# One first store of ten tokens, or two of five, in a mixture-of-experts combine

## The chip, the cores and the metric

The kernel runs on one core of a Trainium2 chip. The metric is device time in microseconds (us) of one execution. Three executions of the kernel before took 239.29, 239.32 and 239.38 us, median 239.32 us. All the other numbers of the kernel before come from one further execution, taken by the hardware profiler.

## The reference

For 16 x 1024 = 16384 tokens there are two expert outputs of 512 floats each and two weights. The result is their weighted sum:

```python
weights = combine_weights[..., np.newaxis]
return np.sum(expert_outputs * weights, axis=2).astype(np.float32)
```

Shapes: `expert_outputs` (16, 1024, 2, 512), `combine_weights` (16, 1024, 2), result (16, 1024, 512), all float32. Two floats are read for each float written: 67.24 MB are read and 33.56 MB written.

## The kernel before

The tokens are laid over the 128 partitions, 128 tokens to each. Tokens 0 to 117 of every partition come from the first part of the input and tokens 118 to 127 from the rest (`LAST`, line 35, and `rows`, line 40). A token takes 4 KB of input and 2 KB of result in its partition.

The partition's 128 tokens are cut into eleven tiles, numbered 0 to 10, of 10, 12, 12, ..., 12 and 10 tokens (`TILES`, line 30). Four rooms in one SBUF tile `et` hold them: tile g lies in room g mod 4 (`ROOMS`, line 29). So tile 4 takes the room of tile 0, tile 5 that of tile 1, and so on.

Three things happen to a tile:

- A load (`load`, line 68, issued on line 71) is one DMA on the queue of SyncE (SP). It has 128 rows, one for each partition; a row of a 12-token tile is 48 KB. Tile 0 alone comes in two loads, of 2 and of 8 tokens (`FIRST`, line 31). The profile calls this queue q1.
- The combine (`combine`, line 76) runs on VectorE (DVE). For tiles 0 to 8 it is one multiply of the whole tile by the broadcast weights (line 83) and one add of the two halves (line 90), which writes the result into the front half of the same room. In tile 9 ScalarE (ACT) does half of the multiplies (lines 87 and 89). In tile 10 ACT and DVE go token by token (lines 95 and 96).
- A store (line 121) is one DMA for each entry of `STORES` (line 32): one each for tiles 0 to 6, one for tiles 7 and 8 together and one for tiles 9 and 10. Stores 0 to 6 are issued by ACT, on its own queue, which the profile calls q10; a row of a 12-token store is 24 KB and a row of store 0 is 20 KB. The last two stores are issued by SP (line 120) and so stand on q1 behind the loads.

After the store of a tile the loop issues the load of the tile four further on (line 124). It takes the same room, so SP waits until that store has wholly landed before it issues the load. SP works its loads strictly in the order of the tiles; while it waits for one store, nothing behind it on SP is issued.

Each DMA signals its end on one of eight completion counters, which the build hands out in turn. A DMA that gets a used counter waits for the counter's previous DMA.

The order of the instructions on each engine is that of the program (`manual_schedule`, line 100). Ahead of the loop stand a small store of zeros (line 104), the two loads of weights (line 74, on q10) and a warm-up of ACT (line 107).

Of the kernel before, what the change touches and what calls it, by code (L numbers as in the profile page):

```python
# [1 line left out]

# [4 lines left out]


@with_exitstack
def kernel(  # L10
    ctx: ExitStack,
    tc: tile.TileContext,
    expert_outputs: bass.AP,
    combine_weights: bass.AP,
    out: bass.AP,
):

    nc = tc.nc
    b, s, k, h = expert_outputs.shape
    assert k == 2
    n = b * s
    P = nc.NUM_PARTITIONS
    per = n // P
    assert per * P == n

    ROOM, ROOMS = 12, 4
    TILES = [10, 12, 12, 12, 12, 12, 12, 12, 12, 12, 10]  # L30
    FIRST = [2, 8, 12, 12, 12]
    STORES = [[0], [1], [2], [3], [4], [5], [6], [7, 8], [9, 10]]
    WHOLE = [0, 1, 2, 3, 4, 5, 6, 7, 8]
    MIXED = [9]
    LAST = 118
    assert sum(TILES) == per and [g for st in STORES for g in st] == list(range(len(TILES)))
    main = per - LAST
    starts = [sum(TILES[:g]) for g in range(len(TILES))]

    def rows(x):  # L40

        first = x[0 : P * main, :].rearrange("(p t) f -> p t f", p=P)
        second = x[P * main : n, :].rearrange("(p t) f -> p t f", p=P)
        return lambda t, c: first[:, t : t + c, :] if t < main else second[:, t - main : t - main + c, :]

    flat = out.rearrange("b s h -> (b s) h")
    eo = rows(expert_outputs.rearrange("b s k h -> (b s) (k h)"))
    cw = rows(combine_weights.rearrange("b s k -> (b s) k"))
    o = rows(flat)

    dt = mybir.dt.float32
    mult = mybir.AluOpType.mult
    add = mybir.AluOpType.add
    copy = mybir.ActivationFunctionType.Copy

    pool = ctx.enter_context(tc.tile_pool(name="all", bufs=1))
    et = pool.tile([P, ROOMS * ROOM, k * h], dt)
    halves = et.rearrange("p j (k h) -> p (j k) h", k=k)
    wt = pool.tile([P, per * k], dt)
    wk = wt.rearrange("p (t k) -> p t k", k=k)  # L60
    zt = pool.tile([16, 128], dt)
    warm = pool.tile([P, 1], dt)

    def place(t):
        g = max(g for g in range(len(TILES)) if starts[g] <= t)
        return g % ROOMS * ROOM + t - starts[g]

    def load(t, c, **kw):
        at = place(t)
        assert place(t + c - 1) == at + c - 1  # L70
        nc.sync.dma_start(out=et[:, at : at + c], in_=eo(t, c), **kw)  # L71

    def weights(q, t, c):
        q.dma_start(out=wk[:, t : t + c, :], in_=cw(t, c))

    def combine(g, base):
        at, c, t0 = g % ROOMS * ROOM, TILES[g], starts[g]
        if g in WHOLE or g in MIXED:
            room = halves[:, k * at : k * (at + c), :]
            x0, x1 = et[:, at : at + c, 0:h], et[:, at : at + c, h : 2 * h]  # L80
            if g in WHOLE:
                wb = wt[:, k * t0 : k * (t0 + c)].unsqueeze(2).to_broadcast([P, k * c, h])
                nc.vector.tensor_tensor(out=room, in0=room, in1=wb, op=mult)  # L83
            else:
                for i in range(c):
                    x = et[:, at + i, 0:h]
                    nc.scalar.activation(out=x, in_=x, func=copy, scale=wt[:, k * (t0 + i) : k * (t0 + i) + 1])  # L87
                w1 = wk[:, t0 : t0 + c, 1:2].to_broadcast([P, c, h])
                nc.vector.tensor_tensor(out=x1, in0=x1, in1=w1, op=mult)  # L89
            nc.vector.tensor_tensor(out=halves[:, base : base + c, :], in0=x0, in1=x1, op=add)  # L90
            return
        for i in range(c):
            t = k * (t0 + i)
            x0, x1 = halves[:, k * (at + i), :], halves[:, k * (at + i) + 1, :]
            nc.scalar.activation(out=x0, in_=x0, func=copy, scale=wt[:, t : t + 1])  # L95
            nc.vector.scalar_tensor_tensor(  # L96
                out=halves[:, base + i, :], in0=x1, scalar=wt[:, t + 1 : t + 2], in1=x0, op0=mult, op1=add
            )

    with tc.manual_schedule():  # L100
        nc.vector.memset(zt, 0.0)  # L101

        ahead = flat[0 : P * main, :].rearrange("(q t) h -> q (t h)", q=16)
        nc.scalar.dma_start(out=ahead[:, 0:128], in_=zt)  # L104
        weights(nc.scalar, 0, main)
        weights(nc.scalar, main, per - main)
        nc.scalar.activation(out=warm, in_=nc.const_aps.tensor(1.0, (P, 1), dt), func=copy)  # L107

        t = 0
        for i, c in enumerate(FIRST):  # L110
            load(t, c, **({"max_dma_last_dim": k * h * 4} if i == 0 else {}))
            t += c
        assert t == sum(TILES[:ROOMS])
        for j, st in enumerate(STORES):
            base, c = st[0] % ROOMS * ROOM * k, 0
            for g in st:
                combine(g, base + c)
                c += TILES[g]
            assert c <= k * ROOM
            q = nc.sync if j in (7, 8) else nc.scalar  # L120
            q.dma_start(out=o(starts[st[0]], c), in_=halves[:, base : base + c, :])
            for g in st:
                if g + ROOMS < len(TILES):
                    load(starts[g + ROOMS], TILES[g + ROOMS])


# [1 line left out]
_INS = ['expert_outputs', 'combine_weights']  # L128
_OUTS = [((16, 1024, 512), 'float32')]


# [23 lines left out]
```

## Time and profile before

| | |
|---|---|
| median of three executions | 239.32 us (239.29 to 239.38) |
| span of the profiled execution, first to last instruction | 237.6 us |
| what an execution has around the span (median less span) | 1.7 us |
| DVE busy | 192.1 us, 81% of the span |
| ACT busy | 15.2 us, 6% |
| DMA moved | 100.80 MB, mean 424 GB/s |

How to read it. The span runs from the first to the last instruction, and all times in the views are counted from its start. The core has 16 DMA engines that move the rows of all DMAs; a record of one row is called a packet. A DMA of 128 rows gives each engine 8 rows, and at its end 16 markers of 4 bytes, one for each engine, which raise the completion counter. So a DMA of 128 rows shows as 144 packets. A queue's share is the time that its packets took, as a share of the time of all 16 engines. "Landing" is the time from the issue of a DMA until its counter is full.

### The profile page before, as it was taken

The numbers are of one execution on the slowest core, as the hardware profiler recorded it, in microseconds if no ns is written. First come the engines' busy times: TensorE is split into PE (matmuls) and PEld (weight loads), VectorE is DVE, ScalarE is ACT, GpSimd is POOL, SyncE is SP. The second block draws the span as 40 slices with busy tenths as digits, with TensorE's granted clock in tenths as the row PEclk, the third lists the DMA queues.
The fourth block names the chain that finished last, engine by engine and source line by source line (L and its number), as shares of the span: only waits on it lengthen the run. The fifth ranks groups of instructions, "written<-read, shape, count | busy, mean of one in ns | idle before, by whom it ended". The sixth has DMA issues, their size and how long they took to land.

```text
span 237.6 us, 154 instructions
## 1 busy us (share of the span) xinstructions
DVE 192.1 (81%) x31; ACT 15.2 (6%) x24; POOL 0.2 (0%) x4
## 2 busy tenths in 40 slices
DVE  0039999999999996998799699969987999998000
ACT  2000000000000000000000000000000008482000
POOL 0000000000000000000000000000000000000000
DMA  7999998999999999999999999999999999999895
GB/s 266 442 445 405 456 481 375 375 430 477 439 447 414 397 405 455 463 397 430 430 505 422 447 414 397 414 447 463 397 439 422 463 404 434 441 463 463 375 485 243
DMA packets 3472, 100.80 MB, mean 424 GB/s; under 512 B 512, under 2 KB 656, under 8 KB 912
## 3 DMA queue, kind: packets, MB, share of 16 engines
q1 hardware_dynamic: 2144, 79.17, 77.6%
q10 hardware_dynamic: 1328, 21.64, 21.2%
HBM read 67.24 MB, written 33.56 MB: 424 GB/s over the span
## 4 chain that ended last, share of the span: by engine, by line
DMA 60%; DVE 30%; issue 1%; DVEq 0%; ACTq 0%; SPq 0%
DMA et<-in_expert_outputs_dram 30%; DMA out_dram<-et 24%; DVE et L83 15%; DVE et L90 10%; DMA wt<-in_combine_weights_dram 6%; DVE et L89 3%; DVE et L96 3%; DVEq L150 0%; ACTq L104 0%; DVE zt L101 0%; SPq L71 0%; DVEq L96 0%; DVEq L83 0%; DVEq L90 0%
## 5 line engine op out<-in xcount | busy, mean ns | idle before, releaser
L83 DVE TENSOR_TENSOR et<-et,wt 128x12288 f32<-128x12288 f32 (+1 forms) x9 | 114.5, 12719 | 25.8 <-DMA wt<-in_combine_weights_dram 14.9
L90 DVE TENSOR_TENSOR et<-et 128x6144 f32<-128x6144 f32 (+1 forms) x10 | 64.5, 6451 | 0.4
L87 ACT ACTIVATE et<-et,wt 128x512 f32<-128x512 f32 x12 | 7.5, 709 | 193.0 <-DMA et<-in_expert_outputs_dram 193.0
L96 DVE SCALAR_TENSOR_TENSOR et<-et,wt 128x512 f32<-128x512 f32 x10 | 6.7, 747 | 0.1
L89 DVE TENSOR_TENSOR et<-et,wt 128x6144 f32<-128x6144 f32 x1 | 6.6, 6552 | 0.0
L95 ACT ACTIVATE et<-et,wt 128x512 f32<-128x512 f32 x10 | 6.2, 707 | 4.7 <-DMA et<-in_expert_outputs_dram 4.7
L107 ACT ACT_TABLE_LOAD x1 | 1.3, 1283 | 2.4 <-issue 2.4
L101 DVE MEMSET zt<- 16x128 f32 x1 | 0.2, 165 | 0.8 <-PEq L139 0.8
L107 ACT ACTIVATE warm<-const-float32-1.0 128x1 f32<-128x1 f32 x1 | 0.2, 203 | 0.0
L139 POOL MEMSET const-bfloat16-1.0<- 128x1 bf16 x1 | 0.1, 101 | 0.0
L139 POOL MEMSET const-uint8-127<- 128x1 uint8 x1 | 0.1, 101 | 0.0
L139 POOL MEMSET const-float32-0.0<- 128x1 f32 x1 | 0.1, 98 | 0.2 <-issue 0.2
L139 POOL MEMSET const-float32-1.0<- 128x1 f32 x1 | 0.1, 98 | 0.0
## 6 DMA issues: line engine op xcount, KB each, us to landing
et<-in_expert_outputs_dram SPq DMA_DIRECT2D x9, 6144.0 KB, 35.3
out_dram<-et ACTq DMA_DIRECT2D x6, 3072.0 KB, 31.9
out_dram<-et SPq DMA_DIRECT2D x1, 6144.0 KB, 24.3
out_dram<-et SPq DMA_DIRECT2D x1, 5632.0 KB, 17.6
et<-in_expert_outputs_dram SPq DMA_DIRECT2D x1, 5120.0 KB, 21.1
et<-in_expert_outputs_dram SPq DMA_DIRECT2D x1, 4096.0 KB, 14.4
out_dram<-et ACTq DMA_DIRECT2D x1, 2560.0 KB, 24.9
et<-in_expert_outputs_dram SPq DMA_DIRECT2D x1, 1024.0 KB, 5.1
```

The lines of the kernel that those rows point to most:

```text
L83: nc.vector.tensor_tensor(out=room, in0=room, in1=wb, op=mult)
L87: nc.scalar.activation(out=x, in_=x, func=copy, scale=wt[:, k * (t0 + i) : k * (t0 + i) + 1])
L89: nc.vector.tensor_tensor(out=x1, in0=x1, in1=w1, op=mult)
L90: nc.vector.tensor_tensor(out=halves[:, base : base + c, :], in0=x0, in1=x1, op=add)
L95: nc.scalar.activation(out=x0, in_=x0, func=copy, scale=wt[:, t : t + 1])
L96: nc.vector.scalar_tensor_tensor(out=halves[:, base + i, :], in0=x1, scalar=wt[:, t + 1 : t + 2], in1=x0, op0=mult, op1=add)
L101: nc.vector.memset(zt, 0.0)
L107: nc.scalar.activation(out=warm, in_=nc.const_aps.tensor(1.0, (P, 1), dt), func=copy)
L139: nc = _bacc.Bacc("TRN2", target_bir_lowering=False, num_devices=1)
```

## The change

Store 0 (tile 0, ten tokens) is issued as two DMAs one behind the other on ACT's queue, the first with tokens 0 to 4 and the second with tokens 5 to 9. Each has 128 rows of 10 KB instead of 128 rows of 20 KB. The other stores keep one DMA each, since there `step` is the whole count.

```diff
             q = nc.sync if j in (7, 8) else nc.scalar
-            q.dma_start(out=o(starts[st[0]], c), in_=halves[:, base : base + c, :])
+            step = c if j else c // 2
+            for i in range(0, c, step):
+                q.dma_start(out=o(starts[st[0]] + i, step), in_=halves[:, base + i : base + i + step, :])
             for g in st:
                 if g + ROOMS < len(TILES):
                     load(starts[g + ROOMS], TILES[g + ROOMS])
```

The load of tile 4 waits for both halves. Because there is one more DMA, the completion counters are handed out differently from there on: the load of tile 3, which shared a counter with the first load of tile 0, now shares it with the small store of zeros.

## The prediction, on record before the result

> **What bounds the kernel now.** I read the page first.
>
> ```profile
> span 237.6 us, 154 instructions
> DVE 192.1 (81%) x31; ACT 15.2 (6%) x24; POOL 0.2 (0%) x4
> ...
> DMA packets 3472, 100.80 MB, mean 424 GB/s; under 512 B 512, under 2 KB 656, under 8 KB 912
> ...
> q1 hardware_dynamic: 2144, 79.17, 77.6%
> q10 hardware_dynamic: 1328, 21.64, 21.2%
> ...
> DMA 60%; DVE 30%; issue 1%; DVEq 0%; ACTq 0%; SPq 0%
> ```
>
> The two queues together hold the 16 DMA engines for 98.8% of the span: all but 2.9 us. DVE, at 81%, has room. The second view cuts the span into stretches; its last two columns are the DMA share and GB/s.
>
> ```profile
> 37.00:57.20 20.20, 20.17 (x3) 0.00 (x0) 0.00 (x0) 1.00 1.05 441
> 57.20:70.80 13.60, 13.56 (x2) 0.00 (x0) 0.00 (x0) 1.00 0.95 408
> 70.80:92.60 21.80, 19.83 (x4) 0.00 (x0) 0.00 (x0) 1.00 1.00 433
> 92.60:199.20 106.60, 97.55 (x11) 2.27 (x4) 0.00 (x0) 1.00 1.00 433
> 199.20:223.50 24.30, 19.77 (x13) 11.42 (x19) 0.00 (x0) 1.00 1.03 447
> ```
>
> Packets count where they start, so 1.05 beside 0.95 is one row over an edge. No stretch leaves the DMA engines idle. Next the chain of waits in order of time (start, length, what), and the waits of DVE and SP (total, times, longest).
>
> ```profile
> 32.30 24.88 DMA out_dram<-et
> ...
> 57.26 35.32 DMA et<-in_expert_outputs_dram
> ...
> 92.60 12.97 DVE et L83
> ```
>
> ```profile
> DVE et L83 <- DMA et<-in_expert_outputs_dram: 10.8, 5, 2.3
> ```
>
> ```profile
> SPq L71 <- DMA out_dram<-et: 169.7, 7, 41.5
> ```
>
> Store 0, the changed one, stands on the chain: it lands at 57.2, then load 4 is issued, lands at 92.6, and DVE, which waits five times about 2.2 us for loads, goes on. Read as a plain chain, a slower store 0 would cost its whole delay. It would be wrong: the 35.3 us of load 4 are mostly time in a queue, as the next part shows.
>
> **How the queues share the engines.** Three stretches of the DMA view (queue: packets, MB, share of 16 engines): 57.3 to 78.9, then 36.9 to 57.2, then 16 to 30.3.
>
> ```profile
> q1 hardware_dynamic: 144, 6.29, 67.3%
> q10 hardware_dynamic: 144, 3.15, 33.8%
> ```
>
> ```profile
> q1 hardware_dynamic: 144, 6.29, 74.2%
> q10 hardware_dynamic: 144, 2.62, 30.0%
> ```
>
> ```profile
> q1 hardware_dynamic: 144, 6.29, 101.7%
> q10 hardware_dynamic: 144, 0.12, 2.5%
> ```
>
> 144 packets to 144, whether the row on q10 has 24 KB, 20 KB or (the weights) 0.9 KB, beside 48 KB on q1: the queues take turns row by row, not byte by byte. Each engine has 8 rows and a marker of a DMA, so a row takes: 48 KB, 67.3% of 21.6 us over 8 = 1.82 us; 24 KB, 33.8% of 21.6 over 8 = 0.913; 20 KB, 30.0% of 20.3 over 8 = 0.761; 0.9 KB, 2.5% of 14.3 over 8 = 0.045. In the Trainium skill, "DMA: Bandwidth & Descriptors", section "Queues, rings and completion order", an engine goes round its queues packet by packet, about 9 to 17 descriptors to a packet. The trace agrees on the turns, with whole rows as the unit; were several rows a turn, the split would alter no share and the sum below would stay.
>
> **The change part by part.** *Bytes and rows.* The bytes stay. Each engine gets 16 rows of 10 KB for 8 of 20 KB, and a second marker. No row of 10 KB is in the trace. From below: the line through 0.761 and 0.913 gives 0.381 for 10 KB, just half, so 0. From above: a 0.9 KB row at the rate of the 20 KB row would take 0.035 and takes 0.045, so 0.010 for each row whatever its size; 8 more rows and a marker make 0.1 us. I take 0.05, the middle, between ends this close. It lies on the path, since the engines are never idle.
>
> *The second issue* on ACT. Its issues of stores (ns each, first and last start), and store 1 alone:
>
> ```profile
> L121 ACTq DMA_DIRECT2D out_dram<-et x7: 338/338/351, 32.3 to 155.8; - x7
> ```
>
> ```profile
> L121 ACTq DMA_DIRECT2D out_dram<-et x1: 351/351/351, 51.8 to 51.8; - x1
> ```
>
> 0.35 us on ACT's queue, where only the wait for store 1 (51.8) stands behind: nothing, hidden by 19 us of waiting. *The counters:* load 3 now waits for the store of zeros in place of the first load.
>
> ```profile
> out_dram<-zt ACTq DMA_DIRECT2D x1, 8.0 KB, 4.1
> ```
>
> That lands about 5.1 us; load 3 is issued a little earlier and queues behind loads 1 and 2 all the same: nothing.
>
> *Store 0 gets later.* Load 3 (issue and landing), and the two queues from 37 to 70.3:
>
> ```profile
> L71 SPq DMA_DIRECT2D et<-in_expert_outputs_dram x1: 328/328/328, 5.9 to 5.9; - x1
> ...
> DMA to landing us min/median/max: 64.9/64.9/64.9
> ```
>
> ```profile
> q1 hardware_dynamic: 221, 9.44, 67.0%
> q10 hardware_dynamic: 237, 4.91, 34.2%
> ```
>
> Load 3 lands at 70.8. From 37 to 70.3 q1 has 9.44 MB, 12 rows and 2 markers for each engine: 14 turns. Beside them q10 took 34.2% of 33.3 = 11.4 us. Now the same 14 turns of q10 carry 13 rows of 10 KB and a marker, 5.0 us. So load 3 lands some 5.5 to 6.4 us earlier (the row under way at 70.3 is the doubt), about 65. Three rows and a marker of store 0 are then left, 1.2 us: it lands about 66.7, not 57.2, and load 4 is issued 9.5 us later.
>
> *What is late next.* From 32.3 to 37 the view has q1 alone:
>
> ```profile
> q1 hardware_dynamic: 32, 1.57, 83.4%
> ```
>
> q1 is empty from 65 until load 4's first row, D after its issue. D is not shown for this case; the nearest rows bound it: the store of zeros, one row to an engine, landed 4.1 us after its issue, which is more than D; store 0, issued at 32.3, had no row before 37 (4.7) behind rows of 48 KB. From below 1. I take 3.5, by the zeros. In that time store 1, issued at 51.8, has both turns: 8 rows of 0.913 from 66.3 to 73.6. So the engines have work until D = 6.9. With D = 3.5 the first row goes at 70.3; before, it went just after load 3's end, about 70.8. From there both queues are full again. Bytes tell the landing: load 4 lands at 92.6 less 0.913 for each row that store 1 is behind where it was. It had 5.8 rows ((4.91 - 2.62) MB are 5.8 rows of 24 KB for each engine), now 2 to 5.7 (D from 1 to 4.7), 4.4 at 3.5. So load 4 lands 0.1 to 3.5 us earlier, not later. DVE can use 1.9 to 2.3 of it, and stores 1 to 6 land 0.2 to 7 us later (1.82 for each row behind).
>
> *The end.* The last two stores, and DVE's last lines in the chain:
>
> ```profile
> out_dram<-et SPq DMA_DIRECT2D x1, 6144.0 KB, 24.3
> out_dram<-et SPq DMA_DIRECT2D x1, 5632.0 KB, 17.6
> ```
>
> ```profile
> 199.25 20.28 SPq L121 DMA_DIRECT2D out_dram<-et  x2
> ```
>
> The first, issued at 199.25, lands at 223.5. The second is issued at 219.2 and lands at 236.8, and its 8 rows of 44 KB (1.67 each) take 13.3 of that: they start at 223.5, right behind the first. So the engines, not DVE, set the end: 4.3 us lie between issue and first row. A DVE that ends 2 us earlier only waits longer there, and the gain is 0.
>
> The sum: 237.6 + 0.05 (0 to 0.1) = 237.65 of span; with the 1.72 us by which the median, 239.32, stands above it, 239.4.
>
> **The rivals.** *A, above: 239.4.* For it: DMA share 1.00 from stretch to stretch. *B, the queues share by bytes,* so that the split does nothing: store 0 lands at about 57.2 as before, 239.3 to 239.4. Against it are the three pairs of 144. *C, load 10 late.* It is issued when store 6 lands:
>
> ```profile
> 187.86 0.33 SPq L71 DMA_DIRECT2D et<-in_expert_outputs_dram  x1
> ...
> 196.93 7.46 ACT L87 ACTIVATE et<-et,wt 128x512 f32<-128x512 f32 x12 [193.04 <-DMA et<-in_expert_outputs_dram]
> ```
>
> Store 6 comes 0.2 to 7 us later. q10 is then empty for good, and load 9 is the last on q1; its landing started ACT at 196.9, so its rows end about 196.4. From 187.9 + lag + D > 196.4 the engines idle for the difference. With one D at both places the sum is 5 to 8 us and 8.5 are there; with 1 at load 4 and 4.3 at load 10 it is 11.3: 2.8 us lost. Middle 1.4: 240.8. For it: the margin is thin. Against: 4.3 is an upper bound.
>
> *D, load 4 late.* If the second half pays a start of its own behind the first, as the 4.1 of the zeros, store 0 lands at 70.8 and load 4's first row goes at 74.3, 0.7 us after store 1 is done. Store 1 is then 2.2 rows ahead: 2.0 and 0.7, so loads 4 to 8 land 2.7 us later, DVE ends at 221.9, not 219.2, and the last store's first row, with 3.5, goes at 225.4, not 223.5: 241.3. It decides from a load that lands 0.8 late, 6.7 rows or D = 5.6 at load 4. Against: ends of DMAs leave no hole in the shares. The Trainium skill, same page, section "Anatomy of one DMA", gives a fixed 2.0 us for each DMA on GpSimd's path, mostly until the last write is confirmed. By that an estimate is 239.3 + 2.0 = 241.3 if it lies on the path; the shares of 1.00 speak against that.
>
> *E, faster.* q1's 8 rows from 36.9 to 57.2 took 74.2% of 20.3 = 15.06 us, 0.5 more than 8 x 1.82: rows drag where store 0 sets in. Other rows may not drag: 238.8. Or they drag once more where q1 sets in again: 239.9. Nothing says which.
>
> **How the numbers follow.** A 0.64, B 0.08, C 0.08, D 0.06, E faster 0.08 and E slower 0.06. 0.2% is 0.48 us, about what a measurement tells from no change. A and B fall within it: 0.72. C, D and E slower make slower 0.20, E faster 0.08. The time is A's, 239.4. The range takes A's 0 to 0.1 with half a drag either way and part of C and D: 239.0 to 240.3; A's own is 239.2 to 239.6.
>
> **What would show it.** Right: store 0's halves land near 55 and 66.7; load 3 lands near 65; SP issues load 4 near 66.7; DVE's waits at line 83 shrink and do not grow; the second last store still lands at 223.5. Wrong: store 0 done by 58 (B); a hole in the DMA share near 196 (C), near 73 or 223 (D); rows longer than 0.39 us for 10 KB.

## The result and the profile after

The changed kernel takes 239.80 us (median of 11 executions, 239.62 to 240.91), the kernel before 239.32 us (11 executions beside them). The ratio is 1.0025, with a 95% interval from 1.0016 to 1.0034: slower by a quarter of a percent, some 0.5 us (the medians alone give 1.0020). The new times also lie further apart: the closest eight of the eleven executions before lie within 0.16 us, those of the change within 0.50. Two single executions of runs below, 243.64 and 242.87 us, were more than 1.5% longer than the fastest of their kernel; they stand in the medians and ranges, but not in the ratios.

The profiled execution of the change has a span of 238.4 us and took 240.16 us, so 1.8 us lie around the span. It is one of the longer ones; its distance to the profile before is 0.8 us, more than the 0.5 us of the medians. The page:

```profile
span 238.4 us, 155 instructions
...
DMA packets 3616, 100.80 MB, mean 423 GB/s; under 512 B 528, under 2 KB 672, under 8 KB 928
...
q1 hardware_dynamic: 2144, 79.17, 77.4%
q10 hardware_dynamic: 1472, 21.64, 21.2%
```

144 packets more, all on q10: 128 rows and 16 markers. The queues hold the engines for 98.6% of a longer span where it was 98.8%, so no hole to speak of has opened. The chain of waits of the change, at the same place as before (start, length, what):

```profile
32.57 33.33 DMA out_dram<-et
...
65.96 27.43 DMA et<-in_expert_outputs_dram
...
93.47 12.97 DVE et L83
```

Store 0 lands at 65.9 where it landed at 57.2, and load 4 needs 27.4 us where it needed 35.3. Most of the delay of 8.7 us is swallowed, as forecast; 0.8 us is not, and load 4 lands at 93.4 where it landed at 92.6. That 0.8 us stays to the end. SP's last line in the timeline of the change:

```profile
200.15 20.28 SPq L123 DMA_DIRECT2D out_dram<-et  x2
```

The second last store is issued 0.9 us later than before and the last one at 220.1, 0.9 later as well.

Where do the 0.8 us come from? Two stretches of the DMA view of the change (queue: packets, MB, share of 16 engines): 66 to 69.6, where q1 is empty, and 69.6 to 70.6, where it comes back.

```profile
DMA packets 64, 1.57 MB, mean 437 GB/s; under 512 B 0, under 2 KB 0, under 8 KB 0
...
q10 hardware_dynamic: 64, 1.57, 101.3%
```

```profile
q1 hardware_dynamic: 10, 0.49, 113.5%
q10 hardware_dynamic: 6, 0.15, 40.3%
```

While q1 is empty, store 1 has all engines, at 437 GB/s: no time is lost there. Then ten engines take a first row of load 4 and six take one more row of store 1. The engines, until then in step, part here. (The records of the rows name no engine; that the same engines are meant further on is read from the counts, ten and six.) The next view is the stretch 69 to 82, first of the kernel before and then of the change.

```profile
q1 hardware_dynamic: 96, 3.93, 69.9%
```

```profile
q1 hardware_dynamic: 78, 3.83, 71.5%
```

Before: 3.93 MB are 80 rows of 48 KB (and 16 markers); 69.9% of 13 us over 16 engines, divided by 80, is 1.817 us, the undisturbed row. After: 3.83 MB are 78 rows; the same sum gives 1.907. The rows drag by 0.09 us each (that is, they take that much longer than the undisturbed row), over the 78 rows 0.44 us for each engine on average. And they do not drag alike. Here are the markers at the end of load 4, which stand under 512 B in the packet line. Before, 91.6 to 92.25:

```profile
DMA packets 32, 0.39 MB, mean 605 GB/s; under 512 B 16, under 2 KB 16, under 8 KB 16
```

After, 90.8 to 91.2 and 92 to 93.1:

```profile
DMA packets 20, 0.25 MB, mean 614 GB/s; under 512 B 10, under 2 KB 10, under 8 KB 10
...
DMA packets 15, 0.27 MB, mean 246 GB/s; under 512 B 6, under 2 KB 6, under 8 KB 6
```

Ten engines are done with load 4 near 91, a microsecond earlier than before, and six only after 92. A DMA has landed when its last engine is done, so load 4 lands with the six. The split has two parts. One is the store row of 0.913 us, which evens out when both queues have passed. The other is the uneven drag, which did not even out to the end: by its markers each engine has the same share of every DMA, so a late one is not relieved by the others. The last markers of the execution show what is left: before, 235.8 to 236.5, and after, 235.9 to 236.5 and 236.5 to 237.5.

```profile
DMA packets 16, 0.00 MB, mean 0 GB/s; under 512 B 16, under 2 KB 16, under 8 KB 16
```

```profile
DMA packets 12, 0.00 MB, mean 0 GB/s; under 512 B 12, under 2 KB 12, under 8 KB 12
...
DMA packets 4, 0.00 MB, mean 0 GB/s; under 512 B 4, under 2 KB 4, under 8 KB 4
```

Twelve engines end where all sixteen ended before, and four end later. The kernel waits for the four. By the start times of these markers in the two traces the mean engine ends only 0.2 us later (236.19 and 236.38) and the last one 0.8 (236.42 and 237.23). So most of the 0.8 us is unevenness, not drag as such. Indeed the kernel before drags as well, only elsewhere (near 35 and near 45.7): over the whole execution its 48 KB rows take 0.83 us more for each engine than rows of 1.815 us would, and those of the change 0.93.

### The profile page after: what moved, and what is told of

Read it like the earlier page. It is cut to its first block, busy times and chain, and to the rows that moved or that the text cites. A ratio compares the mean times of both kernels' runs of the same rounds, so it can differ in the third digit from the quotient of the medians.

```text
span 238.4 us, 155 instructions
## 1 busy us (share of the span) xinstructions
DVE 192.1 (81%) x31; ACT 15.2 (6%) x24; POOL 0.2 (0%) x4
## 4 chain that ended last, share of the span: by engine, by line
DMA 60%; DVE 30%; issue 1%; DVEq 0%; ACTq 0%; SPq 0%
DMA out_dram<-et 28%; DMA et<-in_expert_outputs_dram 26%; DVE et L83 15%; DVE et L90 10%; DMA wt<-in_combine_weights_dram 6%; DVE et L89 3%; DVE et L96 3%; DVEq L152 0%; ACTq L104 0%; ACTq L123 0%; DVE zt L101 0%; DVEq L83 0%; SPq L71 0%; DVEq L96 0%; DVEq L90 0%
## 6 DMA issues: line engine op xcount, KB each, us to landing
out_dram<-et ACTq DMA_DIRECT2D x2, 1280.0 KB, 27.3
```

## The experiments

The theory after the result, called the empty-queue theory: short rows lose turns to the 48 KB rows; so store 0 lands late and load 4 comes too late to follow load 3; q1 runs empty, and when it comes back, rows drag, by amounts that differ from engine to engine and from run to run. Its rivals, the second-DMA theory and the short-row theory: the second DMA costs time by itself, or rows of 10 KB do.

**Store 0 cut by partitions.** Two DMAs, but with the rows of before.

```diff
-            step = c if j else c // 2
-            for i in range(0, c, step):
-                q.dma_start(out=o(starts[st[0]] + i, step), in_=halves[:, base + i : base + i + step, :])
+            step = P if j else P // 2
+            for i in range(0, P, step):
+                q.dma_start(out=o(starts[st[0]], c)[i : i + step], in_=halves[i : i + step, base : base + c, :])
```

> Store 0 in two DMAs as in the change, but cut by partitions: 64 rows of 20 KB each, so each engine has 4 rows and a marker twice. Empty-queue theory (short rows lose turns, store 0 lands late, q1 runs empty, its return drags unevenly over the engines): load 4 is issued near 57.5 as before, q1 never empties, no dragging rows between 64 and 77, 239.3 to 239.4 us. Second-DMA theory (a second DMA costs time by itself): 239.8 us as in the change. Short-row theory (rows of 10 KB cost time themselves): 239.3 us.

Measured: 238.96 us (238.88 to 240.59, 12 executions) beside 239.31; ratio 0.9992, interval 0.9982 to 1.0003. The timeline of SP has load 4 at 58.5, and from 69 to 82:

```profile
58.46 22.16 SPq L71 DMA_DIRECT2D et<-in_expert_outputs_dram  x2
```

```profile
q1 hardware_dynamic: 80, 3.93, 69.8%
```

80 rows at 1.815 us: no drag. A second DMA, with its marker and its issue, costs nothing here. The second-DMA theory falls. The run is even 0.35 us below the kernel before, which no theory had forecast; it comes up again below.

**One DMA with short rows.** The kernel before, with store 0's rows cut to 10 KB inside a single DMA.

```diff
-            q.dma_start(out=o(starts[st[0]], c), in_=halves[:, base : base + c, :])
+            short = {} if j else {"max_dma_last_dim": c // 2 * h * 4}
+            q.dma_start(out=o(starts[st[0]], c), in_=halves[:, base : base + c, :], **short)
```

> Store 0 is one DMA again, but of 256 rows of 10 KB. Empty-queue theory: load 4 is issued near 66, dragging rows between 64 and 77, the engines' markers of load 4 lie over 1.2 us apart, 239.6 to 240.2 us. Second-DMA theory: 239.3 us. Short-row theory: 239.8 us.

Measured: 240.54 us (240.47 to 241.27, 5 executions), ratio 1.0060, interval 1.0048 to 1.0072. It is slower than the change, though it has a DMA less. SP's timeline and the stretch 69 to 82:

```profile
65.76 14.62 SPq L71 DMA_DIRECT2D et<-in_expert_outputs_dram  x2
```

```profile
q1 hardware_dynamic: 78, 3.83, 74.4%
```

Load 4 is issued as late as in the change, and the 78 rows take 1.984 us each: a drag of 0.167 on each, 0.81 us for each engine. The size of the rows does it, not the number of DMAs. Whether the short rows act directly or through the empty queue, the next run tells. Its expectation of 239.6 to 240.2 was too low, and why it loses 1.2 us where the change loses 0.5 stays open.

**The change, with load 4 in two parts.** The back of tile 0's room, from 20 KB on, is free once DVE has added; so tokens 5 to 11 of tile 4 need not wait for store 0.

```diff
             for g in st:
                 if g + ROOMS < len(TILES):
-                    load(starts[g + ROOMS], TILES[g + ROOMS])
+                    t, c = starts[g + ROOMS], TILES[g + ROOMS]
+                    if g == 0:
+                        load(t + 5, c - 5)
+                        c = 5
+                    load(t, c)
```

> The changed kernel with load 4 in two: tokens 5 to 11, whose place in the room no store reads, are issued without waiting for store 0, tokens 0 to 4 after it. Empty-queue theory: q1 keeps rows past 70 while store 0 ends, no dragging rows between 64 and 77, markers 0.6 us apart, 239.3 to 239.5 us (8 more rows and a marker cost 0.1). Second-DMA and short-row theories: 239.8 to 239.9 us.

Measured: 239.16 us (239.09 to 239.45, 11 executions), ratio 0.9996, interval 0.9987 to 1.0004. The short rows and the second DMA are still there, but the extra 0.5 us is gone. Markers at the end of load 4, 91.6 to 92.1:

```profile
DMA packets 32, 0.39 MB, mean 787 GB/s; under 512 B 16, under 2 KB 16, under 8 KB 16
```

All sixteen are there within half a microsecond again. Store 0 lands even later, at 69.2, and it no longer matters, because q1 has rows of load 4 in hand. The short-row theory falls too. The time is a little below the expected 239.3 to 239.5. Once more, in another set:

> The changed kernel with load 4 in two, once more. Empty-queue theory: 239.1 to 239.2 us, no drag between 64 and 77. If the earlier run was a lucky one: 239.6 us or more, with such drags.

Measured: 239.14 us (239.04 to 239.31, 11 executions), ratio 0.9993, interval 0.9984 to 1.0001. The first run was no chance.

**The kernel before, with load 4 in the same two parts.** The control: the same edit without the change.

> The kernel before with load 4 in the same two parts, as the control of the run before. q1 was not empty there, so all theories: 239.3 to 239.5 us.

Measured: 239.45 us (239.27 to 239.82, 11 executions), ratio 1.0010, interval 1.0002 to 1.0019. As expected: the early part gains nothing by itself, so in the run above it was the empty queue that it mended. This run also shows a split that evens out: its markers lie 1.3 us apart at the end of load 4's second part (95.4 to 96.7) and 0.4 at the end of the execution (235.9 to 236.3).

**The change once more**, without an edit, to see how the return of q1 differs.

> The changed kernel once more, for how far the return of q1 differs from run to run. Empty-queue theory: load 4's first rows again come in near 69 to 71, rows drag between 64 and 77 by an amount that differs from the first profile and from engine to engine, the markers of load 4 lie over 1 us apart, 239.6 to 240.9 us. A fixed cost of the change would give the same drags as in the first profile.

Measured: 239.84 us (239.62 to 240.88, 8 executions), ratio 1.0027, interval 1.0015 to 1.0039. This profile has a span of 238.0 us. From 69 to 82, and its last markers, 236 to 236.5 and 236.5 to 237:

```profile
q1 hardware_dynamic: 80, 3.93, 74.1%
```

```profile
DMA packets 11, 0.00 MB, mean 0 GB/s; under 512 B 11, under 2 KB 11, under 8 KB 11
...
DMA packets 5, 0.00 MB, mean 0 GB/s; under 512 B 5, under 2 KB 5, under 8 KB 5
```

The drag is 1.927 less 1.817 on 80 rows, 0.55 us for each engine, more than in the first profile, and yet the execution is 0.4 us shorter: five engines end after the others, but none as late as 237. What counts is the slowest engine, not the mean. Of the 19 executions of the change in its two sets none is below 239.62 us; of the 22 with load 4 in two parts none is above 239.45.

**q1 emptied in another way.** The kernel before with 20 KB rows; loads 4 to 6 are issued behind a store of one token on SP that waits for tile 2. For this, store 2 is cut in two DMAs, one token with rows of 2 KB on SP and the rest on ACT.

```diff
-            q.dma_start(out=o(starts[st[0]], c), in_=halves[:, base : base + c, :])
-            for g in st:
+            t = starts[st[0]]
+            if j == 2:
+                nc.sync.dma_start(out=o(t, 1), in_=halves[:, base : base + 1, :])
+                q.dma_start(out=o(t + 1, c - 1), in_=halves[:, base + 1 : base + c, :])
+            else:
+                q.dma_start(out=o(t, c), in_=halves[:, base : base + c, :])
+            for g in [0, 1, 2] if j == 2 else st if j > 2 else []:
```

> Store 0 as in the kernel before, one DMA of 20 KB rows, but loads 4 to 6 are issued behind a store of one token of tile 2 on SP, which waits for DVE until 71. So q1 runs empty from 70.4 to about 73 with neither short rows nor a second DMA. Empty-queue theory: rows drag between 71 and 80 and the markers of load 4 lie over 1 us apart; loads 4 to 8 land 2 to 4 us later, since store rows take the free turns, and the last store then comes late as well: 240.5 to 243 us. If an empty queue came back without drag: markers 0.6 us apart, 239.4 to 242 us.

Measured: 241.01 us (240.25 to 241.97, 4 executions), ratio 1.0070, interval 1.0044 to 1.0096. The profile is of the longest one, span 240.2 us. Its markers of load 4, 96.2 to 97.3 and 98 to 99.5:

```profile
DMA packets 37, 0.71 MB, mean 648 GB/s; under 512 B 15, under 2 KB 15, under 8 KB 15
...
DMA packets 18, 0.42 MB, mean 279 GB/s; under 512 B 1, under 2 KB 1, under 8 KB 1
```

Fifteen engines are done by 97.3 and one only after 98, and load 4, issued at 71.57, lands at 99.6. So the uneven end comes with store 0 whole as well. But store 2 now has a second DMA with short rows, and the one engine is made late by a row that starts only near the end of load 4, some 16 us behind its first rows near 78.6. This is the stretch 94.5 to 95.6:

```profile
q1 hardware_dynamic: 1, 0.05, 19.0%
```

One row of 48 KB, which took 3.34 us. That the return of q1 is what delays this engine is not shown. Nor does this run separate how much of the 1.7 us belongs to it and how much to loads that simply come later: the two were expected together.

**Two other cuts of store 0.** First 32 partitions in 10 KB rows and 96 in 20 KB rows, then four DMAs of 32 partitions in 20 KB rows.

```diff
-            q.dma_start(out=o(starts[st[0]], c), in_=halves[:, base : base + c, :])
+            for p, n in ((0, 32), (32, 96)) if j == 0 else ((0, P),):
+                short = {"max_dma_last_dim": c // 2 * h * 4} if n == 32 else {}
+                q.dma_start(out=o(starts[st[0]], c)[p : p + n], in_=halves[p : p + n, base : base + c, :], **short)
```

> Store 0 as a DMA of 32 partitions with 10 KB rows and one of 96 partitions with 20 KB rows: 12 turns on each engine, so store 0 lands near 61 and load 4 is queued before load 3 ends. Empty-queue theory: no drag between 64 and 77, 238.9 to 239.3 us. If the drag near 35 belongs to the size of the entering row, it is gone here as in the change, and with the one near 45 gone as in the run by partitions: 238.7 us.

Measured: 239.12 us (238.88 to 243.64, 12 executions), ratio 0.9992, interval 0.9981 to 1.0003. From 69 to 82 it has 80 rows in 69.8%, no drag, with load 4 issued at 62.1; the empty-queue theory holds. The hoped for 238.7 did not come.

```diff
-            q.dma_start(out=o(starts[st[0]], c), in_=halves[:, base : base + c, :])
+            step = P if j else P // 4
+            for i in range(0, P, step):
+                q.dma_start(out=o(starts[st[0]], c)[i : i + step], in_=halves[i : i + step, base : base + c, :])
```

> Store 0 in four DMAs of 32 partitions each with 20 KB rows: 8 rows and 4 markers on each engine, 12 turns. Empty-queue theory: load 4 is issued near 62, before load 3 ends; as the run by partitions, 238.9 to 239.4 us. If each further DMA cost what the change lost: 240.3 us or more.

Measured: 239.29 us (238.99 to 242.87, 13 executions), ratio 1.0010, interval 0.9994 to 1.0026. Three further DMAs do not cost three times what the change lost. The executions lie far apart, and the profile is of the longest of them, 242.87 us, so it does not stand for the others.

**Cut by partitions, once more.**

> The run with store 0 cut by partitions, once more, to tell whether it beats the kernel before: 238.9 to 239.0 us beside 239.3 if the drag near 45 is gone again in the profile; 239.3 if that was chance.

Measured: 238.99 us (238.85 to 240.93, 12 executions) beside 239.32; ratio 0.9995, interval 0.9981 to 1.0010. Both sets have a median some 0.35 us below the kernel before, and both intervals reach over 1, since single executions near 241 stand among them. That this version beats both kernels is likely, not shown.

## Why the prediction was right, and where it was not

The time lies within the range, 239.0 to 240.3, but not within the likeliest case's own 239.2 to 239.6. The forecast of no difference that can be measured does not hold: the ratio's interval begins at 1.0016, 0.4 us. Part of this is luck: the range reached to 240.3 for the sake of C and D, and neither occurred. What came is the time of rival E's slower half, 239.9, to which 0.06 was given, though E has all engines late alike. E's reading of the kernel before was off in place: the 0.5 us that it saw from 36.9 to 57.2 does not lie where store 0's rows set in, at 37.1, but in one row of each engine that starts near 45.7 (the last section shows it).

- *Turn for turn.* Right. q10 had 228 packets beside 213 of q1 from 36.8 to 64.1 in the change:

```profile
q1 hardware_dynamic: 213, 9.44, 81.5%
q10 hardware_dynamic: 228, 2.17, 18.7%
```

- *The price of a row.* Right. In that stretch 2.17 MB are 212 rows of 10 KB (and 16 markers), in 18.7% of 27.3 us over 16 engines: 0.385 us. 16 of them are 6.16 us where 8 rows of 20 KB took 6.09: 0.07, between the bounds of 0 and 0.1.
- *Store 0 gets later, load 3 earlier.* Right. The halves of store 0 land at 53.5 and 65.9 (forecast 55 and 66.7). Load 3, issued at 5.0, lands 59.7 us later, near 64.7 (forecast 65):

```profile
L71 SPq DMA_DIRECT2D et<-in_expert_outputs_dram x1: 327/327/327, 5.0 to 5.0; - x1
...
DMA to landing us min/median/max: 59.7/59.7/59.7
```

- *D, and the cover by store 1.* Right. Load 4, issued at 65.96, has its first rows from 69.6 on, 3.6 us later (taken: 3.5), and q10 had the engines fully until then.
- *"So load 4 lands 0.1 to 3.5 us earlier, not later."* This step failed. It counted bytes on a mean engine and let the rows run at their undisturbed time, and it took the 16 engines for one. Ten engines did as it said and were done near 91, and even the mean of the sixteen markers is 0.4 us earlier than before (91.6 and 92.0); six took another store row and dragged on top, and the landing is theirs. Load 4 came 0.8 us late, and DVE's waits grew where they were to shrink:

```profile
DVE et L83 <- DMA et<-in_expert_outputs_dram: 11.8, 5, 2.9
```

  It was 10.8 us with a longest wait of 2.3.
- *The end is set by the engines, not by DVE.* Right in kind. The markers of the last store show it: twelve engines end as before and four later; the second last store lands at 224.4, not at 223.5. The term that was mis-sized is the sum's "0 to 0.1" for the path: 0.07 for the rows is as forecast; a drag was priced at "half a drag either way" in the range alone, and unevenness between the engines not at all. In this profile the mean engine ends 0.2 us late, rows included, and the unevenness makes the other 0.6.
- *Rival B* falls by the landing of store 0. *Rival C* did not occur: load 10 is issued at 189.5, 1.6 us later, and the DMA share from 92.6 to 199.2 is 1.00:

```profile
92.60:199.20 106.60, 96.66 (x10) 1.44 (x3) 0.00 (x0) 1.00 1.00 433
```

- *Rival D*, a start of its own for the second half, falls: store 0 lands at 65.9, not at 70.8, and the run by partitions loses nothing. So does the estimate of 241.3 from the Trainium skill's 2.0 us for each DMA on GpSimd's path ("DMA: Bandwidth & Descriptors", "Anatomy of one DMA"): with a second DMA and an unchanged row the median is 238.96.

## What to carry to other kernels

Where two queues take turns row by row, the length of a row sets a queue's share: cutting the store's rows in half took its queue from 30.0% of the engines' time to 18.7% while the other queue was full, and whatever waits for that store comes later. Here a delay behind a full queue was free only as long as the queue stayed full; let the next transfer be issued before the one ahead of it ends, by splitting off the part that need not wait. And look at the markers engine by engine: a DMA lands with its slowest engine, and here what unevenness the drag left stayed to the end.

## What was not expected of the hardware

After q1 had been empty and had come back, its 48 KB rows dragged, by 0.44, 0.81 and 0.55 us for each engine in three profiles, though the engines were not idle there. That the return does it rests on the runs in which q1 did not run empty and nothing dragged there; in the second profile of the change most of the drag came only after 77.5, some 8 us behind the return. That an emptied q1 costs the time is shown by the runs with and without it (239.80 and 239.84 beside 239.16 and 239.14); how it makes rows drag, and why unevenly, is open.

Drag alone is no mark of an empty queue. The change has one before q1 runs empty, and the version with load 4 in two parts, which loses nothing, has the same: 61.4 to 62 of the change, and 61.7 to 62.2 of that version's second run:

```profile
q1 hardware_dynamic: 16, 0.79, 355.9%
```

```profile
q1 hardware_dynamic: 16, 0.79, 428.7%
```

Sixteen rows, one on each engine, took 2.13 and 2.14 us each, some 0.3 too long, and all much alike. The kernel before has such a drag too, where no queue had run empty; 45.5 to 46.2 of it, and 44 to 47.3 of the run by partitions:

```profile
q1 hardware_dynamic: 16, 0.79, 330.9%
```

```profile
q1 hardware_dynamic: 16, 0.79, 55.0%
```

Sixteen rows took 2.32 us each there and 1.815 with store 0 cut by partitions, and in the second run of that kernel 1.81 again (56.7% of the stretch 44 to 47.2). This 0.5 us, shared by all engines much alike, is about what that version is faster by. By the times of the markers that follow, the rows near 45.7 are the last of load 2 and those near 61.6 the last of load 3; but the last rows of most loads do not drag, and what makes these wait was not tried.
